# The SwiGLU's output projection as seven products of quarters

## Chip, cores and metric

The kernel runs on one core of one Trainium2 chip (trn2). The metric is the device time of one execution in microseconds, as the median of three runs. The engines are TensorE (PE, matmuls; its weight loads are shown apart as PEld), VectorE (DVE), ScalarE (ACT), GpSimd (POOL), and SyncE (SP), whose queue issues every load and store of the kernel.

## The reference, cut

One layer of a hybrid block over 512 latent tokens and 256 context tokens, width 1024, all float32: a mixer sub-layer (gated linear attention and a short convolution), then a channel sub-layer, then a final norm. The change touches the last lines only; w_in is 1024 x 5632 there and w_out 2816 x 1024:

```
def swiglu(h, w_in, w_out):
    a, b = jnp.split(h @ w_in, 2, axis=-1)
    return (jax.nn.silu(a) * b) @ w_out

x = x + gt2[:, None, :] * swiglu(modulate(rmsnorm(x, g_ffn[l]), sh2, sc2), w_ffn_in[l], w_ffn_out[l])
return rmsnorm(x, g_final)
```

## The kernel before

Matmuls of float32 accuracy are made of three passes of the type float32r: each operand x is split into a high part (a cast to float32r, on ACT) and a low part (x minus the high part, on DVE). `split(src, hi, lo)` issues these two; their line in the profile is L102. `mm3(o, a, b, ...)` issues the passes hi x hi, hi x lo and lo x hi into one PSUM bank; its matmuls stand at L148, whatever calls it. A matmul takes 128 rows of the contraction (a k-tile) and up to 512 columns.

Weights come by `raw_unit` (L117) into one of four `raw` buffers of 1024 columns and are split by `split_raw` into one of four `whi` and four `wlo` buffers. A `Slab` is a list of such pieces.

The hidden layer (tiles f) runs in 11 rounds, `pr`, each with two k-tiles of hidden features: four projections of 8 k-tiles x 3 passes, then `sil` = silu(a) on ACT, times b on DVE (L1157), then `split` of the product into `ah` and `al`. The list `act` ends with 22 pairs, one for each k-tile of the output projection, 128 features x 512 tokens.

The output projection (tiles fo) takes the two column halves `ch` in turn. For each there are 22 k-tiles and four tiles of 128 tokens; the stationary operand is a 128 x 128 piece of `act`, the moving one a 128 x 512 piece of w_ffn_out. The first 14 k-tiles go through all token tiles in turn, the last 8 token tile by token tile, so that the four results are done one after the other. In the second half the last token tile is cut into two banks of 256 columns (fo1l). Behind each result: times the gate (L1182, DVE), plus the residual x1 (L1183, DVE), squares for the final norm with a sum (L1184, ACT), and, in the second half, the norm's factor (sqrt on ACT, reciprocal on DVE), two scalings (L1193 ACT, L1194 DVE) and two stores (L1196, SP).

Buffers come from pools with a fixed number for each tag (`ux` 29, `u2` 10, `uh` 8, `uv` 6, `uo` 8, `hb` 4; PSUM banks: `bank` 3, `gbank` 5). A new tile waits until one of its tag is free. In this part of the kernel nothing is pinned to program order (`pinned` is False from L1148), so the framework's scheduler sets the order on each engine when it builds the program: what is ready and has a buffer, earlier in the program first. On the chip each engine then runs its list in order, with semaphores between the engines.

Of the kernel before, what the change touches and what calls it, by code (L numbers as in the profile page):

```python
# [20 lines left out]
TC = 256
NT = T // P
# [5 lines left out]
FT = DFF // P  # L28
# [18 lines left out]
def hybrid_block(ctx: ExitStack, tc: tile.TileContext, x, c, ctxt, c_ctx, w_ada, b_ada, g_mix, w_in,  # L47
                 w_dec_up, b_dec, g_head, w_gla_out, w_conv, w_conv_out, w_mix_out, g_ffn,
                 w_ffn_in, w_ffn_out, g_final, out):
    nc = tc.nc  # L50
    x, ctxt, out = x[0], ctxt[0], out[0]
    w_ada, w_in, w_gla_out, w_conv_out, w_mix_out = (w[0] for w in (w_ada, w_in, w_gla_out, w_conv_out, w_mix_out))
    w_ffn_in, w_ffn_out = w_ffn_in[0], w_ffn_out[0]

    cst = ctx.enter_context(tc.tile_pool(name="cst", bufs=1))
    wp = ctx.enter_context(tc.tile_pool(name="wp", bufs=3))
    up = ctx.enter_context(tc.tile_pool(name="up", bufs=1))
    sm = ctx.enter_context(tc.tile_pool(name="sm", bufs=4))
# [22 lines left out]
    def ux(name, dt=F32, shape=(P, 512)):  # L81
        return ep.tile(list(shape), dt, tag="ux", name=name, bufs=NX)
# [44 lines left out]
    class Slab:  # L127
# [11 lines left out]
        def at(self, k, cs):  # L139
            (hi, lo), i = self.u[k - self.k0]  # L140
            return hi[:, i, cs], lo[:, i, cs]
# [5 lines left out]
    def mm(*a, **k):  # L147
        pe_pin(nc.tensor.matmul(*a, **k))  # L148
# [4 lines left out]
    def mm3(o, a, b, start, stop):  # L153
        mm(o, a[0], b[0], start=start, stop=False)
        mm(o, a[0], b[1], start=False, stop=False)
        mm(o, a[1], b[0], start=False, stop=stop)

    def rstd_of(ss, n, width, name):

        r = sm.tile([P, n], F32, tag=f"rs{n}", name=f"rs_{name}")  # L160
        act_.activation(r, ss, AF.Sqrt, bias=eps, scale=1.0 / width)
        dve.reciprocal(r, r)
        return r
# [41 lines left out]
    for d in range(2):  # L205
# [9 lines left out]
        mk = cst.tile([P, NT, P], U8, name=f"mask{d}")  # L215
# [4 lines left out]
    for d in range(2):  # L220
        t = cst.tile([P, NT, P], F32, name=f"TP{d}")
# [111 lines left out]
    def proj(slab, j, name, rhs=None, lo=0, n=T, o=None):  # L333

        o = bank(name) if o is None else o
        for _ in proj_steps(slab, j, o, rhs, lo, n):
            pass
        return o
# [15 lines left out]
    pr = [dict(v=[None] * (NC_ + NT)) for _ in range(H)]  # L354
# [169 lines left out]
    for k in range(KT):  # L524
        p_ = k // 2 + 1
# [380 lines left out]
    gates = {}  # L906
# [45 lines left out]
    for pr in range(KT // 2):  # L952
        ada_tick()
        sl_ = Slab(w_in, CCC + pr * 256, 256, f"cc{pr}")
        ccs = []
        for j in range(2):
            o = proj(sl_, j, f"cc{pr}{j}")
            t = ux(f"cc{pr}{j}")
# [3 lines left out]
        sl_ = Slab(w_in, CCH + pr * 256, 256, f"ch{pr}")  # L962
        ucs = []
        for j in range(2):
            ct = 2 * pr + j
            o = proj(sl_, j, f"ch{pr}{j}")
            t = ux(f"u{ct}", F32, (P, ROWS, GW))
            nc.vector.tensor_mul(t, o.rearrange("p (r w) -> p r w", w=GW), ccs[j].rearrange("p (r w) -> p r w", w=GW))
            uc = ux(f"uc{ct}", F32, (P, ROWS, GW))
            w_ = [vec[:, R_WC + i * KT + ct:R_WC + i * KT + ct + 1] for i in range(3)]  # L970
# [5 lines left out]
        sl_ = Slab(w_in, CCB + pr * 256, 256, f"cb{pr}")  # L976
        for j in range(2):
            o = proj(sl_, j, f"cb{pr}{j}")
            t = ux(f"cbu{pr}{j}")
            nc.vector.tensor_mul(t, o, ucs[j].rearrange("p r w -> p (r w)"))  # L980
            hi, lo = ux(f"cuh{pr}{j}", F32R), ux(f"cul{pr}{j}", F32R)
# [13 lines left out]
    for pr in range(KT // 2):  # L995
        ada_tick()
        sl_ = Slab(w_conv_out, pr * 256, 256, f"co{pr}")
        for j in range(2):
            o = proj(sl_, j, f"yc{pr}{j}", rhs=cu)
            nc.vector.tensor_mul(mg[2 * pr + j], o, mg[2 * pr + j])  # L1000
    oghl = []
    for i, t in enumerate(og):
        mk = uv if i < 3 else ux
        hi, lo = mk(f"ogh{i}", F32R), mk(f"ogl{i}", F32R)
# [3 lines left out]
    for pr in range(KT // 2):  # L1008
        ada_tick()
        sl_ = Slab(w_gla_out, pr * 256, 256, f"go{pr}")  # L1010
        for j in range(2):
            i = 2 * pr + j
            o = proj(sl_, j, f"yg{pr}{j}", rhs=oghl)
            t = ux(f"yg{pr}{j}")
            nc.vector.tensor_mul(t, o, sas[pr, j])
            nc.vector.tensor_add(t, t, mg[i])
            hi, lo = ux(f"meh{i}", F32R), ux(f"mel{i}", F32R)
# [11 lines left out]
    x1 = []  # L1029
# [5 lines left out]
    sso = cst.tile([P, NT, 2], F32, name="ssm")  # L1035
# [43 lines left out]
    def mix(t, ch, sl_, after=None):  # L1079
        o = bank(f"mx{ch}{t}")  # L1080
        for k in range(KT):
            mm3(o, tuple(a[:, t * P:(t + 1) * P] for a in me[k]), sl_.at(k, slice(0, 512)), k == 0, k == KT - 1)
            if after and k in after:
                after[k]()
        return o

    for ch in range(2):
        sl_ = Slab(w_mix_out, ch * 512, 512, f"mx{ch}")
# [12 lines left out]
    def steps_of(t):  # L1101

        if t < NT - 1:
            return None

        def a1():
            add2(1, 0)
            ff_split("fa", 0)
            split2(1, 0)

        def a3():
            add2(1, 1)
            ff_split("fa", 1)
            split2(1, 1)

        def a5():
            gains[2]()
            ff_split("fb", 0)
        return {1: a1, 3: a3, 5: a5}
# [3 lines left out]
    for t in range(NT):  # L1123
        o = mix(t, 1, sl_, steps_of(t))
# [11 lines left out]
    act = []  # L1136
    for pr in range(FT // 2):
        if pr == 0:

            todo = [(ff0["fa"], 0), (ff0["fa"], 1), (ff0["fb"], 0), (ff0["fb"], 1)]  # L1140
            obs = [gbank(f"f{pr}{i}") for i in range(4)]
            for c0 in (0, 256):
                for i, ((sl_, j), o) in enumerate(zip(todo, obs)):
                    proj(sl_, j, "", rhs=h2, lo=c0, n=256, o=o)
                    if c0 == 0 and i in (0, 2):
                        turn2(2 + i // 2)
                        shift2(2 + i // 2)
            pinned[0] = False  # L1148
        else:
            fa = Slab(w_ffn_in, pr * 256, 256, f"fa{pr}")  # L1150
            fb = Slab(w_ffn_in, DFF + pr * 256, 256, f"fb{pr}")
            todo = [(fa, 0), (fa, 1), (fb, 0), (fb, 1)]
            obs = [proj(sl_, j, f"f{pr}{i}", rhs=h2) for i, (sl_, j) in enumerate(todo)]
        for j in range(2):
            sil = u2(f"sil{pr}{j}")
            nc.scalar.activation(sil, obs[j], AF.Silu)
            nc.vector.tensor_mul(sil, sil, obs[2 + j])  # L1157
            mk = ux if len(act) < 14 else (uh if len(act) < 18 else (uv if len(act) < 20 else u2))
            hi, lo = mk(f"ah{pr}{j}", F32R), mk(f"al{pr}{j}", F32R)
            split(sil, hi, lo)  # L1160
            act.append((hi, lo))

    gfb = [u2(f"gfb{i}") for i in range(2)]
    for i in range(2):
        nc.sync.dma_start(gfb[i], g_final[i * 512:(i + 1) * 512].partition_broadcast(P))
    sso = cst.tile([P, NT, 3], F32, name="ssf")
    KL = 14
    for ch in range(2):
        sl_ = Slab(w_ffn_out, ch * 512, 512, f"fo{ch}", 0, FT)

        obs = [[((gbank if (t + ch) % 2 else bank)(f"fo{ch}{t}"), 0, 512, 0)] for t in range(NT - ch)]
        if ch == 1:
            obs.append([(mk(f"fo{ch}l{i}"), i * 256, (i + 1) * 256, i) for i, mk in enumerate((bank, gbank))])
        steps = [(k, t, p_) for k in range(KL) for t in range(NT) for p_ in obs[t]]
        steps += [(k, t, p_) for t in range(NT) for p_ in obs[t] for k in range(KL, FT)]
        for k, t, (o, a, e, _) in steps:
            mm3(o[:, :e - a], tuple(w_[:, t * P:(t + 1) * P] for w_ in act[k]), sl_.at(k, slice(a, e)), k == 0, k == FT - 1)
        for t in range(NT):
            for o, a, e, i in obs[t]:
                tmp = u2(f"ft{ch}{t}{i}", F32, (P, e - a))  # L1180
                xv = x1[t][ch][:, a:e]
                nc.vector.tensor_mul(tmp, o[:, :e - a], gates[5][ch][:, a:e])  # L1182
                nc.vector.tensor_add(xv, xv, tmp)  # L1183
                nc.scalar.activation(tmp, xv, AF.Square, accum_out=sso[:, t, ch + i:ch + i + 1])  # L1184
            if ch == 0:
                nc.vector.tensor_mul(x1[t][0], x1[t][0], gfb[0])
            else:
                ss = sm.tile([P, 1], F32, tag="ss", name=f"sf{t}")
                nc.vector.tensor_add(ss, sso[:, t, 0:1], sso[:, t, 1:2])
                if len(obs[t]) == 2:  # L1190
                    nc.vector.tensor_add(ss, ss, sso[:, t, 2:3])
                r = rstd_of(ss, 1, D, f"fin{t}")
                nc.scalar.mul(x1[t][0], x1[t][0], r)  # L1193
                nc.vector.scalar_tensor_tensor(x1[t][1], x1[t][1], r, gfb[1], ALU.mult, ALU.mult)  # L1194
                for i in range(2):
                    nc.sync.dma_start(out[t * P:(t + 1) * P, i * 512:(i + 1) * 512], x1[t][i])  # L1196


# [26 lines left out]
```

## Time and profile before

| | |
|---|---|
| median of three runs | 1009.16 us (1009.11 to 1009.19) |
| the profiled execution's own time | 1009.19 us |
| its span in the profile | 1007.5 us |
| hidden layer, last part / output projection / tail | to 878.7 / 878.7 to 1000.9 / 1000.9 to 1007.5 us |
| PE, DVE, ACT, POOL busy in 878.70 to 1001.00 | 122.18, 40.72, 30.07, 0 us |
| mean granted TensorE clock of the core | 0.998 |

The profile is one execution taken by the hardware profiler. Busy times are the union of an engine's instructions. Durations of single matmuls overlap, since they are pipelined; their pace is read from a run of them.

### The profile page before, as it was taken

The numbers are of one execution on the slowest core, as the hardware profiler recorded it, in microseconds if no ns is written. First come the engines' busy times: TensorE is split into PE (matmuls) and PEld (weight loads), VectorE is DVE, ScalarE is ACT, GpSimd is POOL, SyncE is SP. The second block draws the span as 40 slices with busy tenths as digits, with TensorE's granted clock in tenths as the row PEclk, the third lists the DMA queues.
The fourth block names the chain that finished last, engine by engine and source line by source line (L and its number), as shares of the span: only waits on it lengthen the run. The fifth ranks groups of instructions, "written<-read, shape, count | busy, mean of one in ns | idle before, by whom it ended". The sixth has DMA issues, their size and how long they took to land.

```text
span 1007.5 us, 12881 instructions
## 1 busy us (share of the span) xinstructions
PE 987.3 (98%) x5221; PEld 824.9 (82%) x5221; DVE 546.4 (54%) x845; ACT 382.1 (38%) x602; POOL 2.4 (0%) x10
## 2 busy tenths in 40 slices
PE   6999999999999999999999999999999999999997
PEld 4688888887888888888888888988888888888886
DVE  6678777777556777778443436643333333413424
ACT  5456555558344232224123314633223322311313
POOL 0000000000000000000000000000000000000000
PEclk9999999999999999999999999999999999999999
DMA  9932111112337676667432222242332332331302
GB/s 311 288 88 72 55 38 47 43 42 63 105 121 219 172 218 192 172 187 241 131 103 84 88 80 85 84 126 84 110 99 84 106 104 84 104 126 63 126 21 84
DMA packets 109759, 117.16 MB, mean 116 GB/s; under 512 B 5522, under 2 KB 97796, under 8 KB 109700
## 3 DMA queue, kind: packets, MB, share of 16 engines
q1 hardware_dynamic: 109700, 116.34, 38.0%
q8 instruction: 41, 0.67, 0.3%
q14 instruction: 18, 0.15, 0.0%
HBM read 114.22 MB, written 2.10 MB: 115 GB/s over the span
## 4 chain that ended last, share of the span: by engine, by line
PE 91%; DMA 4%; DVE 2%; ACT 2%; SPq 1%; issue 1%; ACTq 0%
PE f L148 24%; PE fo L148 11%; PE v L148 5%; PE yc L148 4%; PE yg L148 4%; PE gb L148 4%; PE cb L148 4%; PE ch L148 4%; PE cc L148 4%; PE ga L148 4%; PE g L148 4%; PE mx L148 3%; PE o L148 2%; DMA r_w<-in_w_in_dram 2%; PE kl L148 2%; PE q L148 2%
## 5 line engine op out<-in xcount | busy, mean ns | idle before, releaser
L148 PE MATMUL f<-h,h_fa 128*128 128x512 f32 (+1 forms) x384 | 111.1, 372 | 0.2 <-DVE h L102 0.2
L148 PE MATMUL f<-h,h_fb 128*128 128x512 f32 (+1 forms) x384 | 110.3, 372 | 0.0
L148 PEld LDWEIGHTS f<-h,h_fa 128*128 128x128 f32 x384 | 70.2, 188 | 13.3 <-DVE h L102 0.8
L148 PEld LDWEIGHTS f<-h,h_fb 128*128 128x128 f32 x384 | 70.0, 188 | 12.5
L148 PE MATMUL f<-h,l_fb 128*128 128x512 f32 (+1 forms) x192 | 71.3, 371 | 0.0
L148 PE MATMUL f<-h,l_fa 128*128 128x512 f32 (+1 forms) x192 | 71.3, 371 | 0.0
L102 DVE TENSOR_TENSOR l_fa<-r_fa,h_fa 128x1024 fp32r<-128x1024 f32 x22 | 26.9, 1225 | 74.6 <-ACT h_fa L102 74.6
L102 DVE TENSOR_TENSOR l_fo<-r_fo,h_fo 128x1024 fp32r<-128x1024 f32 x22 | 26.9, 1224 | 68.7 <-ACT h_fo L102 68.7
L148 PE MATMUL fo<-h_fo,ah 128*128 128x512 f32 x154 | 60.5, 393 | 0.0
L148 PE MATMUL fo<-l_fo,ah 128*128 128x512 f32 x154 | 60.5, 393 | 0.0
L148 PE MATMUL fo<-h_fo,al 128*128 128x512 f32 x154 | 60.4, 392 | 0.0
L942 DVE SCALAR_TENSOR_TENSOR acc<-r_wa,c,acc 128x256 f32<-128x256 f32 x112 | 54.1, 483 | 8.9 <-DMA r_wa<-in_w_ada_dram 6.1
L102 ACT CAST h_fo<-r_fo 128x1024 fp32r<-128x1024 f32 x22 | 23.1, 1050 | 71.0 <-PE fo L148 27.4
L148 PEld LDWEIGHTS f<-h,l_fb 128*128 128x128 f32 x192 | 36.2, 188 | 6.2
L148 PEld LDWEIGHTS f<-h,l_fa 128*128 128x128 f32 x192 | 36.1, 188 | 6.2
L148 PE MATMUL gb<-h,h_gb 128*128 128x512 f32 x128 | 40.0, 394 | 0.0
L148 PE MATMUL g<-h,h_g 128*128 128x512 f32 x128 | 39.8, 392 | 0.0
L148 PE MATMUL cb<-h,h_cb 128*128 128x512 f32 x128 | 39.7, 391 | 0.0
L148 PE MATMUL ch<-h,h_ch 128*128 128x512 f32 x128 | 39.6, 390 | 0.0
L148 PE MATMUL cc<-h,h_cc 128*128 128x512 f32 x128 | 39.6, 390 | 0.0
L148 PE MATMUL ga<-h,h_ga 128*128 128x512 f32 x128 | 39.4, 390 | 0.0
L1157 DVE TENSOR_TENSOR sil<-sil,f 128x512 f32<-128x512 f32 x22 | 15.1, 688 | 39.7 <-PE f L148 39.7
(319 smaller groups left out, 2276.3 us busy)
## 6 DMA issues: line engine op xcount, KB each, us to landing
r_wa<-in_w_ada_dram SPq DMA_DIRECT2D x32, 512.0 KB, 4.8
r_fa<-in_w_ffn_in_dram SPq DMA_DIRECT2D x22, 512.0 KB, 3.7
r_fb<-in_w_ffn_in_dram SPq DMA_DIRECT2D x22, 512.0 KB
r_fo<-in_w_ffn_out_dram SPq DMA_DIRECT2D x22, 512.0 KB, 3.5
wa<-in_w_ada_dram SPq DMA_DIRECT2D x32, 256.0 KB, 4.8
r_g<-in_w_in_dram SPq DMA_DIRECT2D x8, 512.0 KB, 6.8
r_gb<-in_w_in_dram SPq DMA_DIRECT2D x8, 512.0 KB, 4.0
r_cc<-in_w_in_dram SPq DMA_DIRECT2D x8, 512.0 KB, 4.4
```

Source lines behind the costliest of these rows:

```text
L102: return lambda *a, **k: pin(getattr(self.engine, op)(*a, **k))
L148: pe_pin(nc.tensor.matmul(*a, **k))
L942: nc.vector.scalar_tensor_tensor(acc, w_[:, k, :], ck, acc, ALU.mult, ALU.add)
L1157: nc.vector.tensor_mul(sil, sil, obs[2 + j])
```

## The change

The output projection C = A B is written in quarters. A's rows are cut into two halves of 256 tokens (i), its 22 k-tiles into even and odd ones (j, 11 each); B's columns into two halves (c). With A11 to A22 and B11 to B22, seven products of quarters are formed, each with 11 k-tiles and two token tiles, and C's four quarters are sums of them (Strassen's scheme in Winograd's form):

P1 = A11 B11, P5 = S1 T1, P6 = S2 T2, P3 = S4 B22, P7 = S3 T3, P2 = A12 B21, P4 = A22 T4, with
S1 = A21 + A22, S2 = S1 - A11, S4 = A12 - S2, S3 = A11 - A21,
T1 = B12 - B11, T2 = B22 - T1, T3 = T2 - B11, T4 = B21 - T2.
C11 = P1 + P2, C12 = P1 + P6 + P5 + P3, C22 = P1 + P6 + P7 + P5, C21 = P1 + P6 + P7 + P4 (the code's signs are those of the diff).

The activations stay unsplit (22 tiles of `ux`) and are split for each product by `tokens`. B11 is loaded into eleven tiles `hold`, split for P1, and then overwritten in turn by T1, T2 and T4 (L1152 and following); B12, B22 and again B11 are streamed through the `raw` buffers, two k-tiles at a time; B21 is loaded into three `hb` tiles. T1 to T4 and S2 are computed on POOL, S1, S4 and S3 on DVE. P6 and P3 run in one loop. U holds P1, then P1 + P6, then P1 + P6 + P7; V holds P5. `absorb` applies gate, residual and, where the quarter is the last of its tokens, square, scaling and store; the right column half is finished before the left one.

```diff
         for j in range(2):
-            sil = u2(f"sil{pr}{j}")
-            nc.scalar.activation(sil, obs[j], AF.Silu)
-            nc.vector.tensor_mul(sil, sil, obs[2 + j])
-            mk = ux if len(act) < 14 else (uh if len(act) < 18 else (uv if len(act) < 20 else u2))
-            hi, lo = mk(f"ah{pr}{j}", F32R), mk(f"al{pr}{j}", F32R)
-            split(sil, hi, lo)
-            act.append((hi, lo))
+            a_ = ux(f"a{pr}{j}")
+            nc.scalar.activation(a_, obs[j], AF.Silu)
+            nc.vector.tensor_mul(a_, a_, obs[2 + j])
+            act.append(a_)
...
-    KL = 14
-    for ch in range(2):
-        sl_ = Slab(w_ffn_out, ch * 512, 512, f"fo{ch}", 0, FT)
...
+    KP, HT = FT // 2, T // 2
+    fo = w_ffn_out.rearrange("(r j p) (c b) -> p r j c b", p=P, j=2, b=512)
+    A = [[[act[2 * k + j][:, i * HT:(i + 1) * HT] for k in range(KP)] for j in range(2)] for i in range(2)]
+    U = [uv(f"U{t}") for t in range(2)]
+    V = [uv("V0"), u2("V1")]
...
+    def stream(j, c, name):
+        rs = []
+
+        def at(k):
+            if k % 2 == 0:
+                e = min(2, KP - k)
+                rs.append(wp.tile([P, 2, 512], F32, tag="raw", name=f"r_{name}{k}", bufs=4))
+                nc.sync.dma_start(rs[-1][:, :e], fo[:, k:k + e, j, c, :])
+            return rs[-1][:, k % 2, :]
...
+    def parts(name):
+
+        st = []
+
+        def at(k, src):
+            if k % 2 == 0:
+                st.append([wp.tile([P, 2, 512], F32R, tag=t, name=f"{t}_{name}{k}", bufs=4) for t in ("whi", "wlo")])
+            hl = tuple(w_[:, k % 2, :] for w_ in st[-1])
+            split(src, *hl)
+            return hl
...
+    def tokens(src, name):
+        t = ux(name, F32R)
+        split(src, t[:, :HT], t[:, HT:])
+        return t[:, :HT], t[:, HT:]
+
+    def product(o, a, b, k, ts=(0, 1)):
+        for t in ts:
+            mm3(o[t], tuple(w_[:, t * P:(t + 1) * P] for w_ in a), b, k == 0, k == KP - 1)
...
+    hold = [(uh if k < 8 else uv)(f"hold{k}") for k in range(KP)]
+    for k in range(KP):
+        nc.sync.dma_start(hold[k], fo[:, k, 0, 0, :])
+    w_, o = parts("b11"), banks("P1")
+    for k in range(KP):
+        product(o, tokens(A[0][0][k], f"a11_{k}"), w_(k, hold[k]), k)
+    for t in range(2):
+        nc.scalar.copy(U[t], o[t])
+        absorb(U[t], t, 0, 0)
+
+    r_, w_, o = stream(0, 1, "b12"), parts("t1"), banks("P5")
+    for k in range(KP):
+        nc.gpsimd.tensor_tensor(hold[k], r_(k), hold[k], ALU.subtract)
+        s1 = u2(f"s1_{k}", F32, (P, HT))
+        nc.vector.tensor_add(s1, A[1][0][k], A[1][1][k])
+        product(o, tokens(s1, f"s1p{k}"), w_(k, hold[k]), k)
...
+    o, o3 = banks("P6", bank), banks("P3")
+    for k in range(KP):
+        b22 = r_(k)
+        nc.gpsimd.tensor_tensor(hold[k], b22, hold[k], ALU.subtract)
+        s2 = u2(f"s2_{k}", F32, (P, 2, HT))
+        nc.gpsimd.tensor_tensor(s2[:, 0, :], A[1][0][k], A[1][1][k], ALU.add)
+        nc.gpsimd.tensor_tensor(s2[:, 0, :], s2[:, 0, :], A[0][0][k], ALU.subtract)
+        nc.vector.tensor_sub(s2[:, 1, :], A[0][1][k], s2[:, 0, :])
+        product(o, tokens(s2[:, 0, :], f"s2p{k}"), w_(k, hold[k]), k)
+        product(o3, tokens(s2[:, 1, :], f"s4p{k}"), v_(k, b22), k)
+    for t in range(2):
+        nc.vector.tensor_add(U[t], U[t], o[t])
+    for t in range(2):
+        c12 = summed(U[t], V[t], f"c12{t}")
+        nc.vector.tensor_add(c12, c12, o3[t])
+        absorb(c12, t, 0, 1, True)
...
+        nc.gpsimd.tensor_tensor(b11, hold[k], b11, ALU.subtract)
+        s3 = u2(f"s3_{k}", F32, (P, HT))
+        nc.vector.tensor_sub(s3, A[0][0][k], A[1][0][k])
+        product(o, tokens(s3, f"s3p{k}"), w_(k, b11), k)
...
+    w_, KL, ops, o = parts("t4"), 6, [], banks("P4")
+    for k in range(KP):
+        nc.gpsimd.tensor_tensor(hold[k], b21[k], hold[k], ALU.subtract)
+        ops.append((tokens(A[1][1][k], f"a22_{k}"), w_(k, hold[k])))
+        if k < KL:
+            product(o, *ops[k], k)
+    for t in range(2):
+        for k in range(KL, KP):
+            product(o, *ops[k], k, (t,))
+    for t in range(2):
+        absorb(summed(U[t], o[t], f"c21{t}"), t, 1, 0, True)
```

## Rows read from the trace of the kernel before

**Rows 1.** Page, part 1: engine, busy us, share of the span, instructions.

```profile
PE 987.3 (98%) x5221; PEld 824.9 (82%) x5221; DVE 546.4 (54%) x845; ACT 382.1 (38%) x602; POOL 2.4 (0%) x10
```

**Rows 2.** Chain that ended last, in order of time: start us, us, what.

```profile
779.90 98.83 PE f L148 x436
878.73 62.90 PE fo L148 x273
...
995.13 5.76 PE fo1l L148 x48
1000.89 0.02 issue
1000.92 0.44 DVE ft L1182
...
1001.90 0.52 ACT ft L1184 x2
...
1003.16 0.75 DVE x L1194
```

**Rows 3.** Windows: the output projection's stage, busy us of each engine.

```profile
core 0: us, PE busy (x) PEld busy (x) DVE busy (x) ACT busy (x) POOL busy (x), PEclk, DMA share, GB/s
878.70:1001.00 122.30, 122.18 (x595) 102.40 (x593) 40.72 (x52) 30.07 (x43) 0.00 (x0) 1.00 0.26 86
```

**Rows 4.** Groups by line and form, DVE and ACT, from 700 us on.

```profile
line engine op names shapes xcount | busy us, mean ns | idle before us <-releasers
L102 DVE TENSOR_TENSOR l_fo<-r_fo,h_fo 128x1024 fp32r<-128x1024 f32 x22 | 26.9, 1224 | 68.7 <-ACT h_fo L102 68.7
L102 DVE TENSOR_TENSOR al<-sil,ah 128x512 fp32r<-128x512 f32 x18 | 12.4, 689 | 6.2 <-ACT ah L102 6.2
L1183 DVE TENSOR_TENSOR x<-x,ft 128x256 f32<-128x256 f32 x2 | 0.9, 426 | 0.1
L102 ACT CAST ah<-sil 128x512 fp32r<-128x512 f32 x18 | 11.1, 618 | 43.7 <-DVE sil L1157 43.7
L1184 ACT ACTIVATE ft<-x 128x256 f32<-128x256 f32 x2 | 0.8, 417 | 2.6 <-DVE x L1183 2.6
```

**Rows 5.** Timeline of DVE around the stage's start: start us, us, instruction.

```profile
866.07 1.23 DVE L102 TENSOR_TENSOR l_fo<-r_fo,h_fo 128x1024 fp32r<-128x1024 f32 x1 [6.33 <-ACT h_fo L102]
868.79 1.23 DVE L102 TENSOR_TENSOR l_fo<-r_fo,h_fo 128x1024 fp32r<-128x1024 f32 x1 [1.49 <-ACT h_fo L102]
...
876.95 1.23 DVE L102 TENSOR_TENSOR l_fo<-r_fo,h_fo 128x1024 fp32r<-128x1024 f32 x1 [1.55 <-ACT h_fo L102]
...
879.66 1.23 DVE L102 TENSOR_TENSOR l_fo<-r_fo,h_fo 128x1024 fp32r<-128x1024 f32 x1 [0.20 <-ACT h_fo L102]
880.80 0.68 DVE L102 TENSOR_TENSOR al<-sil,ah 128x512 fp32r<-128x512 f32 x1
```

**Rows 6.** POOL's lines L211 and L213: ns min/median/max, first and last start.

```profile
L211 POOL MEMSET m<- x2: 526/564/601, 1.3 to 3.7; 128x512 f32 x2
L213 POOL TENSOR_SCALAR_AFFINE_SELECT m<-m x2: 294/324/355, 1.9 to 4.4; 128x128 f32<-128x128 f32 x2
```

**Rows 7.** DVE's lines L217 and L240, and the timeline around 4 us.

```profile
L217 DVE CAST mask<-m x8: 208/220/624, 3.6 to 5.2; 128x128 uint8<-128x128 f32 x8
L240 DVE TENSOR_TENSOR sel<-sel,ident x2: 148/194/240, 3.6 to 4.5; 128x2 f32<-128x2 f32 x2
...
3.72 0.60 POOL L211 MEMSET m<- 128x512 f32 x1 [1.52 <-DVE sel L240]
3.78 0.69 DVE L217 CAST mask<-m 128x128 uint8<-128x128 f32 x2
4.39 0.35 POOL L213 TENSOR_SCALAR_AFFINE_SELECT m<-m 128x128 f32<-128x128 f32 x1
4.52 0.24 DVE L240 TENSOR_TENSOR sel<-sel,ident 128x2 f32<-128x2 f32 x1
```

**Rows 8.** Windows: PE busy and granted clock, early and at the end.

```profile
10.00:15.00 5.00, 3.55 (x26) 2.84 (x25) 3.54 (x8) 3.62 (x9) 0.00 (x0) 1.00 1.09 348
1004.00:1007.50 3.50, 0.00 (x0) 0.00 (x0) 0.00 (x0) 0.00 (x0) 0.00 (x0) 0.54 0.40 150
```

More of the change, by code (lines that the diff above doesn't have):

```diff
@@ L1165, in hybrid_block @@
         nc.sync.dma_start(gfb[i], g_final[i * 512:(i + 1) * 512].partition_broadcast(P))
-    sso = cst.tile([P, NT, 3], F32, name="ssf")
-    KL = 14
-    for ch in range(2):
-        sl_ = Slab(w_ffn_out, ch * 512, 512, f"fo{ch}", 0, FT)
[L1171 to L1186, printed above, removed]
-            else:
[L1188 to L1196, printed above, removed]
@@ new lines, in hybrid_block, with banks @@
+    sso = cst.tile([P, NT, 2], F32, name="ssf")
+    KP, HT = FT // 2, T // 2
[3 more added lines that the diff above has]
+    V = [uv("V0"), u2("V1")]
+    def banks(name, mk=gbank):
+        return [mk(f"{name}_{t}") for t in range(2)]
+    def stream(j, c, name):
[6 more added lines that the diff above has]
+            return rs[-1][:, k % 2, :]
+        return at
@@ new lines, in parts @@
+    def parts(name):
[6 more added lines that the diff above has]
+            return hl
+        return at
+    def tokens(src, name):
[5 more added lines that the diff above has]
+            mm3(o[t], tuple(w_[:, t * P:(t + 1) * P] for w_ in a), b, k == 0, k == KP - 1)
@@ new lines, in absorb, with summed @@
+    def absorb(o, t, i, ch, last=False):
+        xv = x1[2 * i + t][ch]
+        tmp = u2(f"ft{i}{t}{ch}")
+        nc.vector.tensor_mul(tmp, o, gates[5][ch])
+        nc.vector.tensor_add(xv, xv, tmp)
+        if last:
+            nc.scalar.activation(tmp, xv, AF.Square, accum_out=sso[:, 2 * i + t, ch:ch + 1])
+            if ch == 1:
+                nc.vector.tensor_mul(xv, xv, gfb[1])
+            else:
+                store(2 * i + t)
+    def summed(a, b, name):
+        tmp = u2(name)
+        nc.vector.tensor_add(tmp, a, b)
+        return tmp
@@ new lines, in store @@
+    def store(t):
+        ss = sm.tile([P, 1], F32, tag="ss", name=f"sf{t}")
+        nc.vector.tensor_add(ss, sso[:, t, 0:1], sso[:, t, 1:2])
+        r = rstd_of(ss, 1, D, f"fin{t}")
+        nc.scalar.mul(x1[t][1], x1[t][1], r)
+        nc.vector.scalar_tensor_tensor(x1[t][0], x1[t][0], r, gfb[0], ALU.mult, ALU.mult)
+        for i in (1, 0):
+            nc.sync.dma_start(out[t * P:(t + 1) * P, i * 512:(i + 1) * 512], x1[t][i])
+    hold = [(uh if k < 8 else uv)(f"hold{k}") for k in range(KP)]
@@ new lines, in hybrid_block @@
+    for t in range(2):
+        nc.scalar.copy(V[t], o[t])
+    r_, w_, v_ = stream(1, 1, "b22"), parts("t2"), parts("b22")
+    o, o3 = banks("P6", bank), banks("P3")
[8 more added lines that the diff above has]
+        product(o3, tokens(s2[:, 1, :], f"s4p{k}"), v_(k, b22), k)
@@ new lines, in hybrid_block @@
+    for t in range(2):
[4 more added lines that the diff above has]
+        absorb(c12, t, 0, 1, True)
+    r_, w_, o = stream(0, 0, "b11"), parts("t3"), banks("P7")
+    for k in range(KP):
+        b11 = r_(k)
+        nc.gpsimd.tensor_tensor(b11, hold[k], b11, ALU.subtract)
+        s3 = u2(f"s3_{k}", F32, (P, HT))
+        nc.vector.tensor_sub(s3, A[0][0][k], A[1][0][k])
+        product(o, tokens(s3, f"s3p{k}"), w_(k, b11), k)
@@ new lines, in hybrid_block @@
+    for t in range(2):
+        nc.vector.tensor_add(U[t], U[t], o[t])
+        absorb(summed(U[t], V[t], f"c22{t}"), t, 1, 1, True)
+    b21 = []
+    for k in range(0, KP, 4):
+        e = min(4, KP - k)
+        t_ = up.tile([P, 4, T], F32, tag="hb", name=f"b21_{k}", bufs=4)
+        nc.sync.dma_start(t_[:, :e], fo[:, k:k + e, 1, 0, :])
+        b21 += [t_[:, i, :] for i in range(e)]
+    w_, o = parts("b21"), banks("P2", bank)
+    for k in range(KP):
+        product(o, tokens(A[0][1][k], f"a12_{k}"), w_(k, b21[k]), k)
@@ new lines, in hybrid_block @@
+    for t in range(2):
+        absorb(o[t], t, 0, 0, True)
+    w_, KL, ops, o = parts("t4"), 6, [], banks("P4")
+    for k in range(KP):
+        nc.gpsimd.tensor_tensor(hold[k], b21[k], hold[k], ALU.subtract)
+        ops.append((tokens(A[1][1][k], f"a22_{k}"), w_(k, hold[k])))
+        if k < KL:
+            product(o, *ops[k], k)
+    for t in range(2):
+        for k in range(KL, KP):
+            product(o, *ops[k], k, (t,))
+    for t in range(2):
+        absorb(summed(U[t], o[t], f"c21{t}"), t, 1, 0, True)
```

## Prediction

> **What bounds the kernel now.** I read the page's busy times first [rows 1]: TensorE (PE) is busy 98% of the span, VectorE (DVE) 54%, GpSimd (POOL) not at all. Then I read the chain of work that ended last, from 780 us on [rows 2]. The reader is to see that it is one unbroken run of PE: the hidden layer's last products (f), then the output projection (fo and its last token tile fo1l) from 878.7 to 1000.9, and only behind it a short tail on DVE and ScalarE (ACT). The first piece gives the pace: 273 matmuls of 512 columns in 62.90 us are 230.4 ns each. (The mean durations of single matmuls, near 390 ns, overlap and can't be summed.) Third, the stage by itself [rows 3]: in 122.30 us PE is busy 122.18, DVE 40.72, ACT 30.07, POOL 0. So PE alone sets this stage, and matmuls taken out of it are worth 230 ns each, as long as the engines that prepare its operands keep up. DVE has 82 us free there; that is the cover the change spends. Last, what one preparation costs [rows 4, 5], and what happens when POOL and DVE work at once [rows 6, 7].
>
> **PE's share.** Before: 22 k-tiles x 4 token tiles x 2 halves x 3 passes = 528 matmuls. After: 7 products x 11 k-tiles x 2 token tiles x 3 passes = 462. The difference is 66 x 230.4 ns = 15.2 us; PE then needs 462 x 230.4 = 106.4 us, or 1.38 us for each k-step of six matmuls.
>
> **DVE's share.** Every operand needs a high part (ACT cast) and a low part (DVE subtraction). Before, the weights were split in 22 pieces of 1024 columns in this stage, the activations once, 22 pieces, in the hidden layer's stage under PE. After, each product splits its own operands, in this stage: 77 weight pieces of 512 columns, 77 token pieces of 256, and 33 sums and differences of 256 columns on DVE (s1, the s4 part of s2, s3: 11 each). Then 40 operations of 512 columns that combine and apply the products (4 behind P1, 12 behind P6 and P3, 10 behind P7, 6 behind P2, 8 behind P4). Durations are 689 ns for 512 columns and 426 ns for 256 [rows 4]; successive ones that don't wait overlap by about 0.09 us (a 1.23 us subtraction starts at 879.66, the next at 880.80) [rows 5]. So I take 0.60 us and 0.33 us: 77 x 0.60 = 46.2, 110 x 0.33 = 36.3, 40 x 0.60 = 24.0, together 106.5 us. With full durations it would be 127 us; that is the upper bound. Without any disturbance DVE thus needs as long as PE: the cover is used up.
>
> **ACT's share.** Of 77 casts of 512 columns and 77 of 256 the first have a row, 618 ns; for the second I take the 417 ns of a 256-column activation [rows 4]: 77 x 1.04 = 80 us, with the copies and squares some 92. That is below 106, beside PE, costed at nothing; uncovered it would be late only if DVE were not later. The splits of the activations that leave the hidden layer's stage (22 x 0.69 us of DVE) win nothing, since PE is the bound there too.
>
> **DMA.** The quarter B11 is loaded twice, 2.9 MB more on the one queue of SP; the DMA engines are busy 0.26 of the stage [rows 3]. Costed at nothing. The waits that are added (raw buffers, `hold` rewritten in place after its split) queue behind SP and POOL with up to eight k-steps of buffer; the b21 loads wait for the h2 tiles, free long before they are needed.
>
> **POOL's share.** It gets t1 to t4, 44 operations of 512 columns, and s2, 22 of 256; as 55 pieces of 512. No row shows a two-input operation on POOL. Nearest from below: a memset of 512 columns, which reads nothing, 526 ns. From above: an affine select of 128 columns, which reads and writes, 294 to 355 ns, four of them 1.18 to 1.42 us [rows 6]. A gain is excluded, as the work is new. I take 1.18 and 0.59 us, because an operation that reads is nearer to the second: 65 us. Alone that would lie beside PE: 11 x 1.18 = 13.0 us in a product of 15.2.
>
> The Trainium skill (GPSIMD Engine Reference, section 3.1) gives 4497 ns for a two-input add of 2048 columns on GpSimd. By an estimate from that page, 1.12 us for 512, the 65 us would be 62.
>
> **Whether POOL lies beside DVE** is the step that decides. In the whole trace they work at the same time only around 4 us [rows 7]. There a memset on POOL runs from 3.72 to 4.32. DVE's eight identical casts (L217) take 208 to 220 ns, except one of 624 ns, which began at 3.78 and so ended at 4.40, as soon as POOL was done. The two-input addition of two columns (L240) takes 148 ns alone and 240 ns beside POOL's select (4.39 to 4.74): it ends at 4.76, again with POOL. So the row says that DVE's instruction doesn't slow a little, it stands until POOL's ends. I therefore add the two engines' times instead of taking the larger.
>
> The Trainium skill (SBUF — State Buffer, section "Who interferes with whom") states the same as a rule that speaks against this change: VectorE and GpSimd share a port pair, and a VectorE instruction with two SBUF inputs and a GpSimd instruction that reads SBUF exclude each other for the whole instruction. The two rows of DVE agree, with 624 against 220 ns and 240 against 148. By that rule the ten DVE operations that have one input in PSUM would escape, which would make the sum 6 us smaller.
>
> **The sum.** DVE 106.5 + POOL 65 = 171.5 us. Some is done before the stage begins: three 1024-column weight splits ran before fo's first matmul at 878.73 and a fourth just after [rows 5], so the four buffers allow eight k-steps of 512; I take 7 us of DVE and 9 us of POOL (eight t1) as early: 155.5. The last eight combining operations (4.8 us) belong to the tail: 150.7 us until the last split. Behind it stand the 18 matmuls that P4's closing loop leaves for the end (the last k-step of token tile 0, 3, and five k-steps of tile 1, 15): 4.1 us. The tail from PE's end to the last result took 3.02 us before (1000.89 to 1003.91) [rows 2]; a whole 512-column tile instead of 256 columns adds 0.27 + 0.27 + 0.21, the extra sum with U 0.73: 4.5 us. Landing of the output as before, 1007.5 - 1003.9 = 3.6. So 878.7 + 150.7 + 4.1 + 4.5 + 3.6 = 1041.6 us of span. The profiled execution took 1009.19 for a span of 1007.5, 1.7 us around it, and agrees with the median of 1009.16: 1043.3. DVE runs in order, so some waits for ACT's high part or for POOL's s2 are exposed; I round up to 1044.
>
> Its own range: with POOL at 0.53 us a piece, 29 less 4 early, the span ends 31 us earlier, 1012; with DVE at full durations (+21) and POOL at 1.42 (+13, less 2 early), 1075.
>
> **Rivals.**
> (a) POOL and DVE don't exclude each other for long operations in SBUF; then it is faster. For it: the only rows of contact are tiny. Against: both DVE rows end with POOL's instruction. Then DVE's 106.5 - 7 - 4.8 = 94.7 and PE's 106.4 run side by side, PE is the later: 878.7 + 106.4 + 4.5 + 3.6 + 1.7 = 994.9; with DVE at full durations it is 127 - 7 - 4.8 = 115 to the last split, and 1008. I take 997. The point: to match 1009.2 the last split must come 1009.2 - 1.7 - 878.7 - 12.2 = 116.6 us into the stage, so DVE may lose 116.6 - 94.7 = 22 us, some 0.4 of POOL's 56. Any more is slower.
> (b) PE's clock falls because PE waits more. For it: the granted clock averages 0.54 from 1004.0 to the end, nearly the 1.2 GHz level, with PE idle since 1000.9. Against: from 10 to 15 us PE was busy only 3.55 of 5 and the granted clock stayed 1.00, that is 2.4 GHz [rows 8]; in this change the gaps would be near 1 us in each k-step. At half the pace 106.4 us would be 213: 878.7 + 213 + 8 + 1.7 = 1101.
> (c) DVE, in order, stands behind POOL's chain t2, s2, s4 in the joint P6/P3 loop, where POOL needs 2.4 us and DVE 2.2 us per k-step, and each hand-over exposes the ACT cast between POOL's result and DVE's subtraction: 0.618 us at each of the 66 operands that POOL feeds (t1 to t4, s2 and s4, 11 each) is 41 us more, 1085. Against it: buffers for eight k-steps, five for the sums.
> (d) The change doesn't save its matmuls. The count of 462 follows from the loops, so I give it nothing.
>
> **How the numbers follow.** Forecast (exclusion, 1012 to 1075): 0.74. (a) 0.17, (b) 0.03, (c) 0.06. The range reaches from 998, which takes in the dearer half of (a), to 1075: 0.74 + 0.08, and 2 in 10 left out. This kernel's measurement can tell 0.2% (2 us) from no change. Faster by more: nearly all of (a), 0.16. Same: 0.02. Slower: 0.82.
>
> **What would show it.** Right: POOL busy near 65 us behind 870; DVE's two-input operations of 512 columns with durations that scatter well above 689 ns, up to near 1.8 us, while POOL works, and 689 where POOL has nothing ready; PE's idle time released by DVE's low parts (L102), its clock still 1.00; the stage 35 to 40 us longer. Wrong: DVE at 689 and 426 ns beside a busy POOL, PE unbroken, the span near 995. POOL's price is read directly from its operations: 1.18 us for 512 columns was my choice between bounds, and with 0.6 us the time would be near 1015.

## Result and the profile after

The changed kernel takes 1045.65 us (median, 1045.07 to 1046.38) against 1009.13 us before: a ratio of 1.036, 95% interval 1.034 to 1.038. It is slower, by 36.5 us; 1044 us had been forecast. The profiled execution took 1045.11 us with a span of 1043.4.

The page's first part answers [rows 1]:

```profile
PE 982.8 (94%) x5085; PEld 814.1 (78%) x5089; DVE 649.9 (62%) x1001; ACT 416.5 (40%) x714; POOL 94.8 (9%) x76
```

PE's busy time has hardly changed in a span that is 36 us longer; DVE has gained 104 us of busy time and POOL 92. Windows of the stage (busy us of each engine, granted clock, DMA) answer [rows 3]; first P1, P5, P6/P3 up to P7's first matmul, then P7, P2 and P4; below them short stretches, the first in front of P5, the others behind the three longest gaps of PE:

```profile
core 0: us, PE busy (x) PEld busy (x) DVE busy (x) ACT busy (x) POOL busy (x), PEclk, DMA share, GB/s
878.70:985.50 106.80, 69.63 (x265) 53.08 (x264) 105.27 (x120) 41.61 (x90) 84.54 (x62) 0.83 0.23 77
985.50:1031.30 45.80, 45.45 (x184) 36.01 (x185) 43.17 (x93) 30.51 (x72) 0.60 (x1) 0.94 0.07 24
...
893.90:903.20 9.30, 0.14 (x1) 0.00 (x0) 9.30 (x10) 2.36 (x6) 6.78 (x5) 0.75 0.19 73
903.20:908.50 5.30, 5.24 (x12) 4.13 (x13) 5.30 (x15) 2.16 (x7) 0.97 (x1) 0.50 0.00 0
948.00:951.50 3.50, 2.93 (x6) 1.82 (x6) 3.50 (x3) 0.41 (x1) 2.53 (x2) 0.50 0.00 0
951.50:955.50 4.00, 3.76 (x9) 2.99 (x10) 4.00 (x10) 0.41 (x1) 0.00 (x0) 0.50 0.23 72
985.50:990.00 4.50, 4.14 (x9) 2.84 (x10) 4.50 (x11) 2.11 (x7) 0.60 (x1) 0.50 0.00 0
```

The reader is to see three things. DVE is busy 105.27 of 106.80 us where POOL works, and again 43.17 of 45.80 where it doesn't: DVE is full throughout. In the first window DVE does 120 instructions, in the second 93 in less than half the time. And PE falls to the 1.2 GHz level (0.50) after the 9.3 us gap in front of P5: 12 matmuls take 5.3 us there, 440 ns each instead of 230. The same level stands behind the gap of 5.4 us that ended at 948 and behind the one of 18.9 us in front of P7.

How one operation fares tells why. Groups by form from 855 us on (busy us, mean ns; then the idle time before), against [rows 4]:

```profile
L102 DVE TENSOR_TENSOR wlo_t<-hold,whi_t 128x512 fp32r<-128x512 f32 x33 | 34.2, 1054 | 0.6 <-ACT whi_t L102 0.5
L1260 POOL TENSOR_TENSOR hold<-r_b,hold 128x512 f32<-128x512 f32 x11 | 20.2, 1859 | 12.7 <-ACT s1p L102 6.8 <-DMA r_b<-in_w_ffn_out_dram 5.8
L1263 POOL TENSOR_TENSOR s<-s,a 128x256 f32<-128x256 f32 x11 | 10.7, 977 | 0.5
L102 DVE TENSOR_TENSOR wlo_b<-b,whi_b 128x512 fp32r<-128x512 f32 x11 | 7.3, 686 | 0.0
...
L1271 DVE TENSOR_TENSOR c<-c,P 128x512 f32<-128x512 f32 x2 | 1.3, 674 | 0.0
```

The first of them once more, by the tile (ns min/median/max, first and last start):

```profile
L102 DVE TENSOR_TENSOR wlo_t<-hold,whi_t x33: 678/687/1783, 888.8 to 1028.3; 128x512 fp32r<-128x512 f32 x33
```

And DVE and POOL in the timeline around 890 us (start us, us):

```profile
888.76 9.14 DVE L102 TENSOR_TENSOR wlo_t<-hold,whi_t 128x512 fp32r<-128x512 f32 x6
890.56 10.13 POOL L1260 TENSOR_TENSOR hold<-r_b,hold 128x512 f32<-128x512 f32 x6
```

The same subtraction of 512 columns takes 686 ns in P2 (wlo_b from B21, POOL idle) and up to 1783 ns beside POOL. Around 890 us six of DVE's run in step with six of POOL's, 1.52 and 1.69 us each. The additions that take one input from PSUM keep to 674 ns although POOL works: c from c and P above, and U from U and P (L1268), which ran beside one of POOL's subtractions (start us, us):

```profile
966.74 1.72 POOL L1299 TENSOR_TENSOR hold<-b,hold 128x512 f32<-128x512 f32 x1
967.25 1.27 DVE L1268 TENSOR_TENSOR U<-U,P 128x512 f32<-128x512 f32 x2
```

What PE waited for, from 878 us on (us in total, times, longest):

```profile
PE P L148 <- ACT s3p L102: 18.9, 1, 18.9
PE P L148 <- ACT s1p L102: 9.2, 1, 9.2
PE P L148 <- DVE wlo_t L102: 5.8, 2, 5.4
```

The gaps are few and long, the longest in front of P7 (s3p) and P5 (s1p). ACT's cast is only the last link: it had waited for DVE's sum, 14.2 us in all for s1 and 8.9 for s3. The end of the chain of waits answers [rows 2]:

```profile
987.04 44.20 PE P L148 x181
1031.24 0.02 issue
1031.26 0.70 DVE c L1224
...
1038.96 0.75 DVE x L1232
```

So the 35.9 us of span come out as: 66 matmuls less, -15.2; PE idle 37.2 + 0.3 in the two windows; PE slower than 230.4 ns a matmul, mostly at the lower clock, 69.6 + 45.5 - (265 + 184) x 0.2304 = 11.6; the tail from PE's last matmul (1034.7) to the end 8.7 instead of 6.6, +2.1. The sum is 36.0.

### The profile page after: what moved, and what is told of

It is laid out like the page before. It is cut to its first block, busy times and chain, and to the rows that moved or that the text cites. A ratio compares the mean times of both kernels' runs of the same rounds, so it can differ in the third digit from the quotient of the medians.

```text
span 1043.4 us, 13035 instructions
## 1 busy us (share of the span) xinstructions
PE 982.8 (94%) x5085; PEld 814.1 (78%) x5089; DVE 649.9 (62%) x1001; ACT 416.5 (40%) x714; POOL 94.8 (9%) x76
## 4 chain that ended last, share of the span: by engine, by line
PE 81%; DVE 10%; DMA 3%; ACT 3%; issue 2%; POOL 1%; SPq 0%; ACTq 0%; DVEq 0%
PE f L148 23%; PE P L148 5%; PE yc L148 4%; PE yg L148 4%; PE gb L148 4%; PE cb L148 4%; PE cc L148 4%; PE ch L148 4%; PE ga L148 4%; PE v L148 4%; PE g L148 4%; PE mx L148 3%; DVE wlo_t L102 2%; PE o L148 2%; PE kl L148 2%; PE q L148 2%
## 5 line engine op out<-in xcount | busy, mean ns | idle before, releaser
L1249 POOL TENSOR_TENSOR hold<-r_b,hold 128x512 f32<-128x512 f32 x11 | 16.4, 1509 | 869.4 <-DVE wlo_b L102 865.7
L102 DVE TENSOR_TENSOR l_fa<-r_fa,h_fa 128x1024 fp32r<-128x1024 f32 x22 | 26.9, 1225 | 79.9 <-ACT h_fa L102 79.9
L102 ACT CAST h_fb<-r_fb 128x1024 fp32r<-128x1024 f32 x22 | 23.1, 1054 | 77.7 <-PE f L148 77.7
L102 DVE TENSOR_TENSOR l_fb<-r_fb,h_fb 128x1024 fp32r<-128x1024 f32 x22 | 26.9, 1224 | 29.3 <-ACT h_fb L102 29.3
L1157 DVE TENSOR_TENSOR a<-a,f 128x512 f32<-128x512 f32 x22 | 15.1, 687 | 37.6 <-PE f L148 37.6
L102 ACT CAST h_fa<-r_fa 128x1024 fp32r<-128x1024 f32 x22 | 23.2, 1053 | 33.1 <-PE f L148 33.1
L148 PE MATMUL v<-h_v,h 128*128 128x256 f32 x192 | 36.3, 285 | 0.0
```

Of the source, the lines that this page charges most:

```text
L102: return lambda *a, **k: pin(getattr(self.engine, op)(*a, **k))
L1157: nc.vector.tensor_mul(a_, a_, obs[2 + j])
L1249: nc.gpsimd.tensor_tensor(hold[k], r_(k), hold[k], ALU.subtract)
```

## Experiments

The theory is the forecast's: a two-input operation of DVE and one of POOL exclude each other, so their times add, and the sum is longer than PE's. The rivals are that POOL lies beside DVE and that DVE's own work, or the order in which it is done, makes the stage long. The kernel before took 1010.0 to 1010.1 us in these runs, against 1009.1 beside the result; each ratio is to it, so a microsecond between runs that were made at different times carries no weight.

### All sums on DVE

```diff
-        nc.gpsimd.tensor_tensor(hold[k], r_(k), hold[k], ALU.subtract)
+        nc.vector.tensor_tensor(hold[k], r_(k), hold[k], ALU.subtract)
```

and likewise in the five other places.

> The 66 two-input operations of POOL (44 of 512 columns, 22 of 256) are issued on DVE instead, nothing else changes. Exclusion (a POOL operation holds DVE's two-input operations up for its whole length): DVE loses POOL's time and gets 44 x 0.60 + 22 x 0.33 = 33.7 us of its own, so the time falls although DVE gets more work: DVE 140 us, less 12 early and 5 in the tail, 1016 us, between 1008 and 1026; durations at 0.69 and 0.42 us everywhere. Rival (POOL lies beside DVE, DVE alone is too slow or badly ordered): 34 us on top of 1045, 1079 us.

Measured: 1027.49 us, ratio 1.017 (1.013 to 1.021). DVE has 34 us more to do and the kernel is 18 us faster. Its operations are back to their own length:

```profile
L102 DVE TENSOR_TENSOR wlo_t<-hold,whi_t 128x512 fp32r<-128x512 f32 x33 | 22.1, 686 | 2.7 <-ACT whi_t L102 2.7
L1277 DVE TENSOR_TENSOR r_b<-hold,r_b 128x512 f32<-128x512 f32 x11 | 7.5, 684 | 0.0
```

The rival that POOL's work was hidden beside DVE is refuted. The time lies just above the 1008 to 1026 that were named; PE still waited 7.6 us for s3p and 3.8 us for s1p.

### The sums left out

```diff
-        nc.gpsimd.tensor_tensor(hold[k], r_(k), hold[k], ALU.subtract)
+        b12 = r_(k)
...
-        product(o, tokens(s1, f"s1p{k}"), w_(k, hold[k]), k)
+        product(o, tokens(s1, f"s1p{k}"), w_(k, b12), k)
```

> The 66 POOL operations are left out: the products take the streamed or held quarter itself in place of T1 to T4 and A21 in place of S2 (so this computes something else), every split, matmul and combining operation stays. Exclusion: DVE is left with 106.5 us and PE with 106.4, both at full pace, 995 to 1003 us, and no gap of PE above 3 us. Rival (DVE's own work, or its order, is what makes the stage long): still above 1030 us.

Measured: 1013.55 us, ratio 1.0027 (1.0011 to 1.0042). Without POOL 32 us are gone, but not the 42 to 50 that were expected: in this order the kernel would be no faster than before even if the sums cost nothing. PE's waits (us in total, times, longest):

```profile
PE P L148 <- ACT s3p L102: 7.2, 1, 7.2
PE P L148 <- ACT s1p L102: 3.8, 1, 3.8
```

DVE's timeline around P5's start:

```profile
895.89 1.28 DVE L1213 TENSOR_TENSOR ft<-U,gt 128x512 f32<-128x512 f32 x2
897.09 1.28 DVE L1214 TENSOR_TENSOR x<-x,ft 128x512 f32<-128x512 f32 x2
898.29 1.09 DVE L1251 TENSOR_TENSOR s<-a,a 128x256 f32<-128x256 f32 x3
899.30 1.09 DVE L102 TENSOR_TENSOR s1p<-s,s1p 128x256 fp32r<-128x256 f32 x3
```

P1 is finished, but DVE first applies it (ft, x: 2.4 us), then makes three s1, and only from these come the cast that PE waits for and the low parts of P5's first operands. The combining operations stand ahead of the next product's operands. That points to a second cause, which the forecast had not priced; the runs on the order below test it.

### POOL busy, but only writing

```diff
-        nc.gpsimd.tensor_tensor(hold[k], b22, hold[k], ALU.subtract)
+        wfill(hold[k])
...
+    def wfill(t):
+        for _ in range(2):
+            nc.gpsimd.memset(t, 0.5)
```

> In place of each POOL operation stand two memsets of the same tile on POOL (the values of T1 to T4 and S2 are thus a constant), some 64 us of POOL work that reads nothing. If it is POOL's reading that excludes DVE's two-input operations: DVE at 0.69 and 0.42 us beside a busy POOL, 995 to 1005 us. If any work of POOL holds DVE up, as the cast of 624 ns beside a memset suggests: near 1040 us, DVE's subtractions again up to 1.2 us.

Measured: 1018.63 us, ratio 1.0086 (1.0057 to 1.0115), 5 us above the run without the sums and 27 below the changed kernel. POOL is busy some 52 us, DVE is not stretched:

```profile
L1171 POOL MEMSET hold<- 128x512 f32 x58 | 29.9, 526 | 26.1 <-DVE wlo_t L102 11.2 <-DVE s1p L102 6.2 <-DVE wlo_b L102 5.5
L102 DVE TENSOR_TENSOR wlo_t<-hold,whi_t 128x512 fp32r<-128x512 f32 x33 | 22.2, 686 | 10.9 <-ACT whi_t L102 10.8
```

So it isn't POOL's being busy that holds DVE's two-input operations up; a POOL that only writes leaves them alone. A memset differs from the sums in its kind and length too, so that it is the reading which counts is the nearest explanation, and no run took it apart from the rest. The time missed the 995 to 1005 that was expected mostly by what the run without the sums missed too, the order. Of the remaining 5 us PE's waits show 2.9, a new one for s2p; the rest stays open.

### Only S2 on DVE

```diff
-        nc.gpsimd.tensor_tensor(s2[:, 0, :], A[1][0][k], A[1][1][k], ALU.add)
-        nc.gpsimd.tensor_tensor(s2[:, 0, :], s2[:, 0, :], A[0][0][k], ALU.subtract)
+        nc.vector.tensor_tensor(s2[:, 0, :], A[1][0][k], A[1][1][k], ALU.add)
+        nc.vector.tensor_tensor(s2[:, 0, :], s2[:, 0, :], A[0][0][k], ALU.subtract)
```

> Only the 22 operations of 256 columns (S2) move from POOL to DVE; T1 to T4 stay on POOL. Exclusion, as a dose: POOL loses 22 x 0.8 to 0.95 = 17 to 21 us, DVE gains 22 x 0.33 = 7 us, so 10 to 14 us less than 1045: 1033 us. Rival (POOL beside DVE): 7 us more, 1052 us.

Measured: 1047.57 us, ratio 1.037 (1.034 to 1.040). The expected 10 to 14 us did not come. POOL's line L1277 (T3; ns min/median/max, first and last start):

```profile
L1277 POOL TENSOR_TENSOR r_b<-hold,r_b x11: 1257/1704/11547, 946.2 to 987.4; 128x512 f32<-128x512 f32 x11
```

The timeline of the two engines from 946 us on:

```profile
946.23 12.98 POOL L1277 TENSOR_TENSOR r_b<-hold,r_b 128x512 f32<-128x512 f32 x2 [9.74 <-DVE s L1263]
946.62 0.41 DVE L1264 TENSOR_TENSOR s<-a,s 128x256 f32<-128x256 f32 x1
946.95 0.41 DVE L102 TENSOR_TENSOR s2p<-s,s2p 128x256 fp32r<-128x256 f32 x1
947.29 0.68 DVE L102 TENSOR_TENSOR wlo_b<-r_b,whi_b 128x512 fp32r<-128x512 f32 x1
...
956.80 1.25 DVE L102 TENSOR_TENSOR s4p<-s,s4p 128x256 fp32r<-128x256 f32 x1 [0.19 <-ACT s4p L102]
```

One POOL subtraction lasted 11.5 us. Beside it DVE issued one two-input operation after another at its full pace (0.41 and 0.68 us), and POOL came through only when DVE first had to wait, at 956.6. This is the exclusion seen from the other side: here DVE kept what POOL needed. The dose itself did arrive: what DVE's operations took above their own lengths fell from 52 to 36 us (counted from 855 us on, as in the part on why below). But the chain that ended last runs through T3 and T4 on POOL from 946 to 978 us, DVE stood idle 17 us in place of 7 from 878.7 on, PE waited 23.4 us for s3p instead of 18.9, and the gain was lost again. That the two engines' times add says nothing about which of them is served. What decides between alternation, as around 890 us in the changed kernel, and this starving stays open.

### The order: combining operations deferred

Three runs with the same edit: each product's combining operations are issued five k-steps (four in P4) into the next product.

```diff
-        absorb(U[t], t, 0, 0)
+    late = [lambda: [absorb(U[t], t, 0, 0) for t in range(2)]]
+
+    def flush(k, at=5):
+        if k == at:
+            late.pop()()
...
+        flush(k)
         product(o, tokens(s1, f"s1p{k}"), w_(k, hold[k]), k)
```

> As the run without POOL's sums (so it computes something else), but each product's combining operations on DVE are issued five k-steps into the next product, behind its first operands. Theory (what is left of the loss without POOL is DVE's order: PE waited 3.8 us before P5 and 7.2 us before P7, both times while DVE worked through combining operations, and PE's clock fell behind both): the two gaps shrink below 2 us each and the clock stays, 1013.5 - 9 - 5 = about 1000 us. Rival (DVE's total is the bound, so that the order only moves the gap): no gain, above 1010 us.

Measured, without the sums: 1000.64 us, ratio 0.990 (0.988 to 0.992). The gaps have closed, and the mean granted clock of the core is 0.997 instead of 0.991:

```profile
PE P L148 <- ACT s3p L102: 1.1, 1, 1.1
PE P L148 <- DVE wlo_b L102: 0.5, 1, 0.5
```

Where DVE's total fits beside PE's, the order was worth 13 us.

> As the run with all sums on DVE (1027.5 us), with the same deferral. There DVE has 140 us of work against PE's 106, so its total is the bound and the order can win only the clock: 1018 to 1026 us. Rival (order is what costs there too): 1013 us or less.

Measured, with all sums on DVE: 1023.62 us, ratio 1.013 (1.011 to 1.015), 4 us less than in the old order (two runs each). DVE is busy 119.1 of the 121.3 us from 878.7 to 1000 there: its total is the bound.

> The changed kernel with POOL's sums as they are, and only the combining operations deferred by five k-steps. Theory (with POOL the bound is DVE's time plus POOL's, so the order can't win what it won without POOL, 13 us): 1036 to 1045 us, DVE and POOL again stretched. Rival (the order of DVE is the main cause, exclusion only adds to it): 1030 us or less.

Measured, the changed kernel with only the deferral: 1044.01 us, ratio 1.033 (1.031 to 1.035). PE's wait for s1p falls from 9.2 to 1.6 us and that for s3p from 18.9 to 10.2, yet the kernel wins only 1.6 us by the medians, 2.6 measured against the kernel before, and the intervals of the two ratios overlap: other waits (11.4 us for DVE's low parts of weights, 6.9 before) take their place, the mean granted clock of the core is no better (0.977 for 0.978), and DVE is stretched as before:

```profile
L102 DVE TENSOR_TENSOR wlo_t<-hold,whi_t 128x512 fp32r<-128x512 f32 x33 | 34.8, 1060 | 0.0
```

Beside POOL, then, closing a gap wins little: PE's gaps and its slow clock are mostly the consequence, and the two engines' common time is the bound.

### A version with the weights' sums made ahead

T1 to T4 hang on weights alone. They can be made in the hidden layer's stage, where DVE has room, be stored, and be streamed like weights:

```diff
+    def weight_sums(k):
...
+            nc.sync.dma_start(q[j, c_], fo[:, k, j, c_, :])
+        b11, b12, b21, b22 = q[0, 0], q[0, 1], q[1, 0], q[1, 1]
+        nc.vector.tensor_sub(b12, b12, b11)
+        nc.vector.tensor_sub(b22, b22, b12)
+        nc.vector.tensor_sub(b11, b22, b11)
+        nc.vector.tensor_sub(b21, b21, b22)
+        for i, t in enumerate((b12, b22, b11, b21)):
+            nc.sync.dma_start(TS[i][k // 2][:, k % 2, :], t)
```

> T1 to T4 depend on weights alone: here DVE computes them in the hidden layer's stage, where it is idle 60% of the time, one k-tile in each of the 11 rounds (44 x 0.60 = 26 us of DVE, under PE), stores them to memory (11.5 MB) and the products stream them like weights. S2 is on DVE, POOL does nothing, the combining operations are deferred as above. The result is the full computation. DVE then has 106.5 + 7.3 = 114 us for the stage, less 8 early and 5 in the tail, about 101, PE 106.4: PE is the bound again, 878.7 + 106.4 + 4.5 + 3.6 + 1.7 = 995 us, with small gaps 996 to 1004, faster than before. Rival (the added loads, stores and DVE work disturb the hidden layer's stage, or DVE still comes late): first matmul of P1 after 885 us, or above 1009 us.

Measured: 1018.90 us, ratio 1.0083 (1.0066 to 1.0100). The rival held: P1 began only at 892.6 us. The new loads didn't start with their rounds but as soon as a buffer was free (first, last start):

```profile
L1146 SPq DMA_DIRECT2D q<-in_w_ffn_out_dram x44: 328/430/925, 521.9 to 640.8; - x44
```

All of them stood between 522 and 641 us, in the mixer's last part, where DVE waited 23.6 us for them and PE then for DVE (mx 3.0 us) and for h (3.9 us). The next run holds each round's loads back by one column written from that round's activation (and starts a round earlier, with two k-tiles in the first round):

```diff
+            nc.vector.tensor_copy(q[j, c_][:, 0:1], after[:, 0:1])
             nc.sync.dma_start(q[j, c_], fo[:, k, j, c_, :])
```

> As the run with the sums ahead in the hidden layer's stage, but each round's loads are held back by an operation of one column that reads this round's activation, so that none of it starts before that round (there the first began at 521 us, before the mixer had ended, and the hidden layer came 14 us late). Theory: the first matmul of P1 is back at 879 to 881 us, and the time is 1018.9 - 13 = 1004 to 1007 us, slightly faster than before. Rival (the extra transfers of 23 MB or DVE's 26 us are what costs, wherever they lie): above 1012 us.

Measured: 1008.05 us, ratio 0.9977 (0.9968 to 0.9987), a microsecond above the 1004 to 1007 that were expected. The loads lie between 665 and 861 us, and P1's first matmul is at 879.5 (two tiles' lines):

```profile
L1147 SPq DMA_DIRECT2D q<-in_w_ffn_out_dram x44: 327/382/778, 665.0 to 860.5; - x44
L148 PE MATMUL P<-whi_b,a x88: 388/393/405, 879.5 to 981.6; 128*128 128x512 f32 x88
```

The same 23 MB of traffic and 26 us of DVE hold the hidden layer up by a microsecond at most in the right place: PE is busy 213.70 of the 213.70 us from 665.0 to 878.7, as before. The last run also moves P2 ahead of P7.

> As the held run, and P2, whose operands need the least of DVE (0.93 us a k-step against PE's 1.38), is put between the joint loop P6/P3 and P7, so that the twelve combining operations behind P6/P3 fall into it. Theory: the gap before P7 (3.2 us) goes, 1000 to 1004 us. Rival (the gap moves to the front of P7 or P2): no difference to the held run.

Measured: 1006.42 us, ratio 0.9963 (0.9949 to 0.9977), 0.4% faster than the kernel before and the lowest time of a version that computes the whole result, but above the 1000 to 1004 that were expected. The wait for s3p falls from 3.2 to 2.3 us, but 2.2 us for wlo_t appear; the intervals of the two runs overlap, so what P2's place is worth isn't settled. Window of the stage:

```profile
878.70:1000.00 121.30, 110.74 (x465) 86.22 (x463) 109.58 (x237) 74.49 (x169) 0.00 (x0) 1.00 0.44 150
```

PE is busy 111 us and DVE 110: of the 15.2 us of matmuls saved some 4 are won, and they are paid for with a DVE that is as full as PE.

## Why the prediction was right, and where it wasn't

**PE's share** was right: 462 matmuls, and at full clock (990 to 1018 us) 120 of them in 28.0 us, 233 ns each.

**DVE's share** was nearly right: in the deferred run without the sums DVE is busy 103.8 us from 878.7 to 1000, where the forecast had 106.5 less 7 early, 99.5; the lengths there are 0.69 and 0.42 us. **ACT** and **DMA** were hardly ever late by themselves: PE waited 1.7 us for a cast of s2, and POOL 5.8 us for a streamed b22 tile.

**POOL's price** was too low. The shortest operations, taken as those that had no wait inside them, took 1.26 us (512 columns) and 0.79 us (256) against 1.18 and 0.59: 44 x 1.26 + 22 x 0.79 = 72.8 instead of 65 us. The estimate of 1.12 us from the Trainium skill (GPSIMD Engine Reference, section 3.1) was further off. Busy time, with the waiting inside it, was 92 us.

**Exclusion** was right, and it is what decided. Five groups of DVE in the changed kernel (wlo_t from hold and from r_b, a, s4p, L1264), each taken as its count times what its mean lies above that in the run without sums or with all sums on DVE (0.687 and 0.419 us), give 12.1 + 4.3 + 6.5 + 4.3 + 4.3 = 31.5 us, and all groups some 52 (from 855 us on; 49 from 878.7 on). The forecast had put 56 us of POOL (65 - 9 early) on DVE's path. The lengthened operations show the exclusion directly, and the POOL operation of 11.5 us shows it from POOL's side; moving the sums to DVE, or leaving POOL nothing to read, takes the lengthening away. The rule of the Trainium skill (SBUF — State Buffer, "Who interferes with whom") agrees with them, and with the write-only run in that a memset doesn't stand in a two-input operation's way (686 ns). One reading behind the forecast was wrong all the same: of its two rows of contact [rows 7] only the addition (240 ns beside a select that reads) is a case of that rule. The cast of 624 ns has one input and lay beside a memset, which reads nothing, and the write-only run shows that a memset says nothing of two-input operations.

**The sum** came out within 2 us, in part by luck. The last split was forecast for 1029.4 and ended at 1028.95 (1028.27 + 0.68), but the terms of that stretch of 150 us were off: DVE was busy 148.4 us in it, 49 of them lengthening by POOL (56 in the forecast) and so some 99 its own work (94.7), and it was idle for 2 (none). The two errors cancel. Behind it PE's rest was 5.8 us, not 4.1, the tail 5.0 (1034.7 to 1039.7) for 4.5, the landing 3.7 for 3.6. And what lay between was not as told. I had DVE late in every k-step by a microsecond, up to the end. In fact DVE and POOL bind up to 985.5, with most of PE's gaps gathered in front of P5 and P7, and in P7, P2 and P4, where POOL had finished, PE and DVE are both full. POOL's too low price and the operations from PSUM, which I had counted as excluded too, pull in opposite directions as well: the four of them that met a reading POOL (U, L1268, and c, L1271) took 674 ns, as the same section of the Trainium skill has it for a single SBUF input.

**Rival (a)** was rightly held unlikely, but its price was wrong: 997 us, against 1013.6 without the sums and 1018.6 with a POOL that only writes. The step that failed is that DVE's combining operations were added to its total as if their place didn't matter. Standing ahead of the next product's operands they cost 13 us of gaps and clock (1013.6 against 1000.6, both without the sums).

**Rival (b)** was dismissed for a reason that didn't hold: gaps near 1 us in each step. There were gaps of 5.4, 9.2 and 18.9 us, and the clock did fall to 0.50 behind each. The 11.6 us that PE lost, mostly by it, are not on top of the sum, since DVE was full meanwhile; closing most of the first gap in the changed kernel, and half of the second, won only some 2 us.

**Rival (c)** didn't show as a chain of hand-overs: POOL waited 12.7 us in all at L1260, beside a DVE that was hardly ever idle.

**The signs named**: DVE's lengths up to near 1.8 us (1.783) and 686 ns in P2 came as said, and the stage is some 34 us longer, for 35 to 40. POOL was said to be busy near 65 us and was for 92, the waiting included. PE's waits were said to end with DVE's low parts (L102); most ended with ACT's casts of s1 and s3, behind DVE's sums. The clock was said to stay at 1.00, and did not.

## What to carry to other kernels

An idle engine is only worth what it can do while the busy one works: before moving elementwise work to POOL, look in the trace for any moment at which both read, and if the one stands until the other ends, add their times; the same sums were cheaper on the full DVE than on the idle POOL. A scheme that saves matmuls moves the cost to what prepares their operands, so count that per k-step against PE, and put whatever combines a finished product behind the next one's first operands (13 us where DVE had room, some 2 beside POOL). What depends on weights alone can be made in an earlier stage that has room, if its loads are tied to that stage.

## What the runs showed that was not expected

A single POOL operation of 512 columns can last 11.5 us instead of 1.26 beside an unbroken train of DVE operations; the profile shows it as busy all that time, so POOL's 92 us of busy time are no measure of its work. PE's granted clock was 0.50 for 5.3 us behind a gap of 9.3 us (12 matmuls at 440 ns), 0.50 from 948.0 to 955.5 behind a gap of 5.4, and 0.50 from 985.5 to 990.0 behind the gap of 18.9, so that a long gap costs PE twice. And a memset on POOL, which had held a DVE cast for 624 ns in [rows 7], left DVE's two-input operations alone at 686 ns.
